# A hybrid attention block: which PSUM pool holds the weighted sums of the cross attention, and where Silu's table is loaded

## The chip, the cores and the metric

The kernel runs on one core of a Trainium2 chip. The metric is the device time of one launch in microseconds (us). The core has five engines with instruction queues of their own, each of which works strictly in order: TensorE (PE in the profile, with its weight loads as PEld), VectorE (DVE), ScalarE (ACT), GpSimdE (POOL) and SyncE (SP), which here issues the transfers.

## What is computed

One layer of an encoder on 1024 tokens of width 1024: a mixer (windowed attention and a gated delta rule), a cross attention of 4 heads into 256 memory tokens, and a SwiGLU feed-forward part. The change touches the cross attention alone:

```python
def _memory_cross_attention(h, mem_n, w_q, w_kv, w_o):
    q = (h @ w_q).reshape(b, s, CROSS_HEADS, CROSS_HEAD_DIM)
    kv = mem_n @ w_kv                       # k, v: 256 memory tokens, 4 heads of 256
    p = jax.nn.softmax(jnp.einsum('bqhd,bkhd->bhqk', q, k) * (CROSS_HEAD_DIM ** -0.5), axis=-1)
    o = jnp.einsum('bhqk,bkhd->bqhd', p, v).reshape(b, s, D_MODEL)
    return o @ w_o
```

All matrix products are made to almost float32 accuracy from float32r parts: an operand is split into a high part (a rounding cast, on ACT) and a low part (the source less the high part, on DVE or POOL), and a product is three matmuls, high x high, high x low and low x high.

## The kernel before

The sequence is worked in two halves of 512 tokens, `hf` 0 and 1; with 4 heads that makes 8 rounds (half, head), called heads 0 to 7 below. The helper `split` (L102 the high part, L103 the low part) and `load_w` (L127 the load into `wraw`, then the split into `whi` and `wlo`) serve everywhere.

For each round the loop calls `cross_q`, which makes q for one head (tile `pcq`, two column tiles of 24 matmuls 128x512, the dense product, L263), and then `cross_attention` for the round before. That has these steps on the way: scores into `pcs` (L1110, 24 matmuls 128x256, two tiles of 12 for two pairs of token tiles), row maxima (`cmx`, L1112 and L1113, DVE), exponentials (`cpr`, L1117, ACT), sums inverted and multiplied in (L1119, L1120, DVE), 8 transposes on PE into two tiles `pct` (L1126), their split into `cph` and `cpl`, the weighted sums `pco` (L1136, two tiles of 6 matmuls) and their split, which overwrites q. After the last round a Silu over a tile of 4 columns (L1151) makes ACT load the table of Silu, which the feed-forward part needs first at L1233. What follows is the output product `mid_gemm` with `w_co`, first for half 0 and then for half 1 (tile `pmg`, L1021, 192 matmuls each); its first lines load the gain `gpost` (L995) and multiply it by 32 on ACT (L996).

PSUM has eight banks, in three pools at this stage: `pg3`, tag `pg`, 4 banks, which `pcq` and `pmg` take in turn; `pn3`, tag `pn`, 2 banks, for the transposes `ptn` and `pct`; `px3`, tag `px`, 2 banks, for `pcs` and `pco`. A tile takes over a bank when the last reader of the tile before it is done.

The order of the work on each engine isn't written out: the framework's scheduler takes the instructions by priority (that is, by their place in the program, with loads of weights ahead) as soon as its model of time finds inputs, an engine and a buffer free, and fixes one order per engine when the kernel is built. Within a pool's tag, banks are given in the order of the requests. An edit of one line can therefore move instructions on every engine.

Of the kernel before, what the change touches and what calls it, by code (L numbers as in the profile page):

```python
# [10 lines left out]
F32 = mybir.dt.float32  # L11
F32R = mybir.dt.float32r
I32 = mybir.dt.int32
AF = mybir.ActivationFunctionType
# [5 lines left out]
P = 128  # L20
S = 1024
D = 1024
KT = D // P
# [52 lines left out]
def tile_hybrid_block(  # L76
# [6 lines left out]
    nc = tc.nc  # L83
# [9 lines left out]
    def f32(ap):  # L93
        return ap.bitcast(F32)

    def bc(ap, axis, shape):
        return ap.unsqueeze(axis).to_broadcast(list(shape))

    def split(hi, lo, src, scale=None, eng=None):

        if scale is None:
            nc.scalar.copy(hi, src)  # L102
            (eng or nc.vector).tensor_tensor(lo, src, f32(hi), ALU.subtract)  # L103
        else:
            nc.scalar.activation(hi, src, AF.Identity, scale=scale)
            nc.vector.scalar_tensor_tensor(lo, src, scale, f32(hi), ALU.mult, ALU.subtract)

    def pool(name, bufs, **kw):
        return tc.tile_pool(name=name, bufs=bufs, reuse_waits="tile", **kw)
# [84 lines left out]
    pg = pgs.enter_context(pool("pg", 3, space=PSUM))  # L194
# [769 lines left out]
    pg = p3.enter_context(pool("pg3", 4, space=PSUM))  # L964
    pn = p3.enter_context(pool("pn3", 2, space=PSUM, side="right"))
    px = p3.enter_context(pool("px3", 2, space=PSUM, side="right"))
# [132 lines left out]
    def cross_attention(q, h):  # L1099
        prs = []  # L1100
        mxs = tx.tile([P, 4], F32, tag="cmx", name="cmx")
        sums = tx.tile([P, 4], F32, tag="csum", name="csum")
        for tp in range(2):
            pp = px.tile([P, 2, ML], F32, tag="px", name="pcs")
            for t2_ in range(2):
                tt = slice((2 * tp + t2_) * P, (2 * tp + t2_ + 1) * P)
                for j in range(2):
                    ct = 2 * h + j
                    for i, (a, b_) in enumerate(((0, 0), (1, 0), (0, 1))):
                        nc.tensor.matmul(pp[:, t2_, :], q[a][:, ct, tt], kr_[b_][:, ct, :],  # L1110
                                         start=(j == 0 and i == 0), stop=(j == 1 and i == 2))
            nc.vector.tensor_reduce(mxs[:, 2 * tp:2 * tp + 2], pp, axis=AX.X, op=ALU.max)  # L1112
            nc.vector.tensor_scalar(mxs[:, 2 * tp:2 * tp + 2], mxs[:, 2 * tp:2 * tp + 2], -1.0 / 16.0, None, ALU.mult)  # L1113
            pr = tx.tile([P, 2, ML], F32, tag="cpr", name="cpr", bufs=4)
            for t2_ in range(2):
                n = 2 * tp + t2_
                nc.scalar.activation(pr[:, t2_, :], pp[:, t2_, :], AF.Exp, bias=mxs[:, n:n + 1], scale=1.0 / 16.0,  # L1117
                                     accum_out=sums[:, n:n + 1])
            nc.vector.reciprocal(sums[:, 2 * tp:2 * tp + 2], sums[:, 2 * tp:2 * tp + 2])  # L1119
            nc.vector.tensor_tensor(pr, pr, bc(sums[:, 2 * tp:2 * tp + 2], 2, (P, 2, ML)), ALU.mult)  # L1120
            prs.append(pr)
        pts = []
        for kt in range(2):
            pt = pn.tile([P, 512], F32, tag="pn", name="pct")
            for t in range(4):
                nc.tensor.transpose(pt[:, t * P:(t + 1) * P], prs[t // 2][:, t % 2, kt * P:(kt + 1) * P], ident)  # L1126
            ph = tx.tile([P, 512], F32R, tag="cph", name="cph", bufs=2)
            pl = tx.tile([P, 512], F32R, tag="cpl", name="cpl", bufs=2)
            split(ph, pl, pt)
            pts.append((ph, pl))  # L1130
        for j in range(2):
            po = px.tile([P, 512], F32, tag="px", name="pco")
            cs = slice((2 * h + j) * P, (2 * h + j + 1) * P)
            for kt in range(2):
                for i, (a, b_) in enumerate(((0, 0), (0, 1), (1, 0))):
                    nc.tensor.matmul(po, vr_[a][:, kt, cs], pts[kt][b_], start=(kt == 0 and i == 0),  # L1136
                                     stop=(kt == 1 and i == 2))
            split(q[0][:, 2 * h + j, :], q[1][:, 2 * h + j, :], po)
        return sums

    q0, behind = operand(opB, "s1"), None
    for hf in range(2):
        q = operand(opB, "s2") if hf else q0
        for h in range(4):
            cross_q(hf, q, h)
            if behind:
                cross_attention(*behind)
            behind = q, h
    q1 = q
    last = cross_attention(*behind)  # L1150
    nc.scalar.activation(last, last, AF.Silu)  # L1151
    L2.close()
    Lk.close()

# [87 lines left out]
    pg = L0.enter_context(pool("pg4", 8, space=PSUM))  # L1242
# [298 lines left out]
```

## Time and profile before

| what | value |
|---|---|
| median of 3 runs | 1548.82 us (1545.64 to 1549.28) |
| profiled execution | 1551.7 us, of which the profile's span is 1549.9 us |
| PE busy | 1494.9 us (96% of the span) |
| DVE / ACT / POOL busy | 1060.1 / 713.3 / 302.6 us |
| mean granted TensorE clock | 0.986 |
| scores `pcs` of the cross attention | from 671.7 to 859.5 us |
| weighted sums `pco` | from 713.9 to 869.5 us |
| Silu's table load | 1283 ns, at 863.1 us |

Times in the profile are counted from the start of the span. A row of the timeline gives the start, the length, the engine, the line, the operation with its output and inputs, the count of merged instructions, and in brackets the idle time before it with what ended it. A row of a table by stage gives for a stretch its length, then for each engine busy time and count, then the granted clock of TensorE, the share of the transfer engines and GB/s. A matmul's length overlaps with the next one's: dense matmuls 128x512 follow each other every 0.23 us, though each is listed with 0.39 us.

### The profile page before, as it was taken

How to read it: one execution, taken by the hardware profiler on the slowest of the kernel's cores; microseconds unless marked ns; L12 is line 12 of the kernel's file. 1: busy time of each engine (PE TensorE's matmuls, PEld its weight loads, DVE VectorE, ACT ScalarE, POOL GpSimd, SP SyncE). 2: the span in 40 equal slices, each digit the busy share in tenths (PEclk: the TensorE clock that was granted, in tenths of full speed). 3: DMA queues.
4: the chain of work that ended last, by engine and by line, in shares of the span. 5: the costliest groups of instructions: out<-in, count | busy, mean ns of one | idle time of the engine just before them, and what ended most of it. 6: DMA issues, size and time to landing. Idle time of an engine off the chain costs nothing.

```text
span 1549.9 us, 20928 instructions
## 1 busy us (share of the span) xinstructions
PE 1494.9 (96%) x7451; PEld 1257.4 (81%) x7451; DVE 1060.1 (68%) x1762; ACT 713.3 (46%) x1377; POOL 302.6 (20%) x297
## 2 busy tenths in 40 slices
PE   6999999988999999999999999999999999999998
PEld 5888887877899878888888777888888888888786
DVE  6877898756898766443346377786868554696676
ACT  5665552236556765454334554322323332454532
POOL 2000110000003202253202231443433433000010
PEclk9999999999999999999999999999999999999999
DMA  6244456767997585354223264344433334853355
GB/s 206 74 131 124 133 150 164 209 169 246 317 305 244 161 294 173 117 181 149 69 69 130 72 205 142 112 136 129 148 119 121 102 102 147 289 189 102 109 175 165
DMA packets 267366, 247.16 MB, mean 159 GB/s; under 512 B 39016, under 2 KB 204797, under 8 KB 267261
## 3 DMA queue, kind: packets, MB, share of 16 engines
q1 hardware_dynamic: 267261, 245.82, 50.8%
q8 instruction: 59, 0.97, 0.3%
q14 instruction: 46, 0.38, 0.1%
HBM read 173.65 MB, written 69.50 MB: 157 GB/s over the span
## 4 chain that ended last, share of the span: by engine, by line
PE 80%; DMA 7%; DVE 6%; ACT 3%; SPq 2%; issue 2%; POOL 1%; DVEq 0%; ACTq 0%; POOLq 0%
PE pg L263 13%; PE pmg L1021 9%; PE pD L1212 8%; PE pE L1212 8%; PE pA L1212 7%; PE pcq L263 6%; PE pdX L1402 6%; PE pdA L1402 4%; PE pB L1212 4%; PE psc L787 2%; PE pdD L1402 2%; PE pco L1136 1%; PE pcs L1110 1%; PE pdX L1495 1%; DVE wlo L103 1%
## 5 line engine op out<-in xcount | busy, mean ns | idle before, releaser
L102 ACT CAST whi<-wraw 128x1024 fp32r<-128x1024 f32 x108 | 113.4, 1050 | 149.7 <-PE pg L263 36.0
L263 PE MATMUL pg<-hhi,whi 128*128 128x512 f32 x352 | 142.1, 405 | 2.8 <-DVE rop L732 2.8
L263 PE MATMUL pg<-hlo,whi 128*128 128x512 f32 x352 | 141.0, 401 | 0.0
L263 PE MATMUL pg<-hhi,wlo 128*128 128x512 f32 x352 | 140.7, 400 | 0.0
L103 DVE TENSOR_TENSOR wlo<-wraw,whi 128x1024 fp32r<-128x1024 f32 x78 | 95.4, 1224 | 63.4 <-ACT whi L102 62.3
L1021 PE MATMUL pmg<-whi,b 128*128 128x512 f32 x384 | 118.6, 393 | 0.2 <-ACT b L102 0.2
L1212 PE MATMUL pA<-s,whi 128*128 128x512 f32 x352 | 109.5, 392 | 1.2 <-ACT m L1229 1.0
L103 POOL TENSOR_TENSOR wlo<-wraw,whi 128x1024 fp32r<-128x1024 f32 x30 | 72.3, 2411 | 146.6 <-ACT whi L102 146.4
L1021 PEld LDWEIGHTS pmg<-whi,b 128*128 128x128 f32 x384 | 71.5, 188 | 14.7 <-ACT b L102 0.6
L263 PEld LDWEIGHTS pg<-hhi,whi 128*128 128x128 f32 x352 | 67.8, 193 | 16.9 <-DVE rop L732 3.3
L263 PEld LDWEIGHTS pg<-hhi,wlo 128*128 128x128 f32 x352 | 68.0, 193 | 13.5
L263 PEld LDWEIGHTS pg<-hlo,whi 128*128 128x128 f32 x352 | 67.9, 193 | 13.4
L1212 PEld LDWEIGHTS pA<-s,whi 128*128 128x128 f32 x352 | 65.4, 188 | 15.2 <-ACT m L1229 1.5
L1402 PE MATMUL pdX<-dhl,whi 128*128 128x512 f32 x264 | 76.1, 390 | 1.5 <-DVE zv L1457 0.8
L1021 PE MATMUL pmg<-wlo,b 128*128 128x512 f32 x192 | 72.2, 391 | 0.0
L1212 PE MATMUL pA<-s,wlo 128*128 128x512 f32 x176 | 68.6, 391 | 1.8 <-DVE wlo L103 1.8
L102 ACT CAST whi<-araw 128x1024 fp32r<-128x1024 f32 (+1 forms) x36 | 35.3, 982 | 70.8 <-PE pdX L1402 27.6
L1289 POOL TENSOR_TENSOR act<-act,up 128x512 f32<-128x512 f32 x33 | 50.1, 1519 | 88.5 <-DVE up L1288 53.2
L103 DVE TENSOR_TENSOR wlo<-araw,whi 128x1024 fp32r<-128x1024 f32 (+1 forms) x36 | 40.8, 1133 | 38.7 <-ACT whi L102 36.2
L288 DVE SCALAR_TENSOR_TENSOR acc<-cp,cols,acc 128x1024 f32<-128x1024 f32 x48 | 61.4, 1281 | 1.5 <-ACT acc L286 0.8
L1402 PEld LDWEIGHTS pdX<-dhl,whi 128*128 128x128 f32 x264 | 49.3, 188 | 12.8 <-issue 1.1
L1262 DVE TENSOR_TENSOR sr<-sr,wraw 128x512 f32<-128x512 f32 x22 | 36.6, 1662 | 28.6 <-POOL sr L1261 28.6
(410 smaller groups left out, 3963.9 us busy)
## 6 DMA issues: line engine op xcount, KB each, us to landing
wraw<-in_w_gate_up_dram SPq DMA_DIRECT2D x52, 512.0 KB, 3.9
kv<-d_kv SPq DMA_DIRECT2D x32, 512.0 KB, 6.9
wraw<-in_w_in_dram SPq DMA_DIRECT2D x22, 512.0 KB, 4.9
b<-in_w_down_dram SPq DMA_DIRECT2D x20, 512.0 KB, 7.4
araw<-d_as SPq DMA_DIRECT2D x20, 512.0 KB, 3.9
pz<-d_pz SPq DMA_DIRECT2D x32, 256.0 KB, 7.1
wraw<-in_w_ckv_dram SPq DMA_DIRECT2D x16, 512.0 KB, 7.0
wraw<-in_w_out_dram SPq DMA_DIRECT2D x16, 512.0 KB, 3.9
```

The costliest lines, as they stand in the source:

```text
L102: nc.scalar.copy(hi, src)
L103: (eng or nc.vector).tensor_tensor(lo, src, f32(hi), ALU.subtract)
L263: nc.tensor.matmul(p_, w[:, k, :], ah[a][:, k, :], start=(k == 0 and i == 0), stop=(k == nk - 1 and i == 2))
L288: nc.vector.scalar_tensor_tensor(acc, cp[:, t:t + S], taps[t], acc, ALU.mult, ALU.add)
L787: nc.tensor.matmul(out[:, d, h, :], lt[:, d, h, :], rt[:, d, h, :], start=True, stop=True)
L1021: nc.tensor.matmul(pp[t], act[a][:, k, tt], w_[:, kk, :], start=(k == 0 and i == 0), stop=(k == KT - 1 and i == 2))
L1110: nc.tensor.matmul(pp[:, t2_, :], q[a][:, ct, tt], kr_[b_][:, ct, :], start=(j == 0 and i == 0), stop=(j == 1 and i == 2))
L1136: nc.tensor.matmul(po, vr_[a][:, kt, cs], pts[kt][b_], start=(kt == 0 and i == 0), stop=(kt == 1 and i == 2))
L1212: nc.tensor.matmul(out_, w[a][:, k, :], xx[b_][:, k, :], start=(start and k == 0 and i == 0), stop=(k == HK - 1 and i == 2), skip_group_ch ...
L1262: nc.vector.tensor_tensor(s[1], s[0], a_[:, 0:HK], ALU.subtract)
L1289: nc.gpsimd.tensor_tensor(o_, o_, up, ALU.mult)
L1402: nc.tensor.matmul(banks[t], a[:, k - k0, tt], w, start=(first and k == 0 and i == 0), stop=(k == NB - 1 and i == 2), skip_group_check=not ...
```

## The change

Two lines differ. The weighted sums take their bank from the pool `pg3`, the one of the dense products, where they took it from `px3`. And the small Silu reads the high part of the last column tile of q for half 1, which the last split of the last round writes; before, it read and wrote the sums of the softmax.

```diff
         for j in range(2):
-            po = px.tile([P, 512], F32, tag="px", name="pco")
+            po = pg.tile([P, 512], F32, tag="pg", name="pco")
             cs = slice((2 * h + j) * P, (2 * h + j + 1) * P)
...
     last = cross_attention(*behind)
-    nc.scalar.activation(last, last, AF.Silu)
+    nc.scalar.activation(last, f32(q1[0][:, KT - 1, 0:4]), AF.Silu)
```

PE executes the same matmuls and transposes in both. The first 3106 in the built programs stand in the same order, up to the scores of head 0 (685.6 us in the trace of before); then the orders differ up to the 4095th, in the middle of the second output product; from there on they are the same again. What the built programs show at three places follows. Numbers at the end of a tile's name tell tiles of one name apart; `x2` is a row that stands twice.

**ACT, the first round of the cross attention.** `ptn` are the transposes of half 1's normalized input and `s00` its high part; `cpr_6981` and `cpr_7001` are the exponentials of head 0, `cpr_7125` and `cpr_7145` those of head 1, `pcq_7048` and `pcq_7081` the dense product of head 2. Before:

```order
L105 ACTIVATE s00_6754<-ptn_6791,cols_73 128x512
L102 CAST whi_7188<-wraw_7186 128x1024
L102 CAST b0_6830<-pcq_7048 128x512
L105 ACTIVATE s00_6754<-ptn_6798,cols_73 128x512
L105 ACTIVATE s00_6754<-ptn_6805,cols_73 128x512
L102 CAST whi_7221<-wraw_7219 128x1024
L102 CAST b0_6830<-pcq_7081 128x512
L1117 ACTIVATE cpr_6981,csum_6965<-pcs_6966,cmx_6964 128x256 x2
L996 ACTIVATE gpost_8001<-gpost_8001 128x1024
L1117 ACTIVATE cpr_7001,csum_6965<-pcs_6986,cmx_6964 128x256 x2
```

With the change:

```order
L105 ACTIVATE s00_6754<-ptn_6791,cols_73 128x512
L105 ACTIVATE s00_6754<-ptn_6798,cols_73 128x512
L105 ACTIVATE s00_6754<-ptn_6805,cols_73 128x512
L996 ACTIVATE gpost_8001<-gpost_8001 128x1024
L1117 ACTIVATE cpr_6981,csum_6965<-pcs_6966,cmx_6964 128x256 x2
L1117 ACTIVATE cpr_7001,csum_6965<-pcs_6986,cmx_6964 128x256 x2
L1117 ACTIVATE cpr_7125,csum_7109<-pcs_7110,cmx_7108 128x256 x2
L102 CAST cph_7011<-pct_7006 128x512
L102 CAST cph_7020<-pct_7015 128x512
L1117 ACTIVATE cpr_7145,csum_7109<-pcs_7130,cmx_7108 128x256 x2
```

The casts of head 2's product are gone from between, and the scaling of `gpost` stands ahead of all exponentials of head 0. On PE the transposes `ptn_6784` to `ptn_6805` stand directly behind the scores of head 0, and behind them the scores of head 1 (`pcs_7110`, then `pcs_7130`), the transposes `pct` of head 0 and its first `pco`; the dense product of head 2 comes after these. On SP the load of `gpost` and four loads of `xr` stand ahead of the load of `wraw_7332`, which they followed before.

**PE, a round in the middle.** `pct_7294` and `pct_7303` are the transposes of head 2, `pcq_7659` belongs to head 6, `pcq_7338` to head 4. Before:

```order
L263 MATMUL pcq_7659<-s01_6755,whi_7655 128x512
L263 MATMUL pcq_7659<-s00_6754,wlo_7656 128x512
L1126 MATMUL pct_7294<-ident_68,cpr_7269 128x128 x2
L1126 MATMUL pct_7303<-ident_68,cpr_7269 128x128 x2
L263 MATMUL pcq_7659<-s00_6754,whi_7655 128x512
L263 MATMUL pcq_7659<-s01_6755,whi_7655 128x512
L1126 MATMUL pct_7294<-ident_68,cpr_7289 128x128 x2
L1126 MATMUL pct_7303<-ident_68,cpr_7289 128x128 x2
L263 MATMUL pcq_7659<-s00_6754,wlo_7656 128x512
```

With the change:

```order
L1110 MATMUL pcs_7420<-kr0_6007,b0_6830 128x256
L1110 MATMUL pcs_7420<-kr0_6007,b3_6831 128x256
L1110 MATMUL pcs_7420<-kr1_6008,b0_6830 128x256
L1126 MATMUL pct_7294<-ident_68,cpr_7269 128x128 x2
L1126 MATMUL pct_7303<-ident_68,cpr_7269 128x128 x2
L1126 MATMUL pct_7294<-ident_68,cpr_7289 128x128 x2
L1126 MATMUL pct_7303<-ident_68,cpr_7289 128x128 x2
L1136 MATMUL pco_7312<-cph_7299,vr0_6009 128x512
L1136 MATMUL pco_7321<-cph_7299,vr0_6009 128x512
L263 MATMUL pcq_7338<-s00_6754,whi_7334 128x512
```

Before, the dense products run some four heads ahead and stand between all steps of a head, and in half 1 the output product of half 0 takes that place. With the change the 16 scores that are left of head 2 and all 24 of head 3 stand in a row of 40, the transposes of head 2 and two of its weighted sums follow at once, and the dense product is at most two heads ahead. This pattern comes for heads 2 and 3, 4 and 5, and 6 and 7. No matmul of the output product stands among the scores any more; its first 21 come just before the last ten `pco` of head 7.

**DVE and ACT, the last rounds.** `pcs_7832` and `pcs_7852` are the scores of head 6, `pcs_7910` and `pcs_7930` those of head 7, `pcq_7803` the last dense product, `wlo_8049` a weight of the output product. DVE with the change:

```order
L1112 TENSOR_REDUCE cmx_7830<-pcs_7832 128x2
L103 TENSOR_TENSOR wlo_8049<-wraw_8046,whi_8048 128x1024
L103 TENSOR_TENSOR b2_7331<-pcq_7803,b1_7330 128x512
L1113 TENSOR_SCALAR cmx_7830<-cmx_7830 128x2
L1112 TENSOR_REDUCE cmx_7830<-pcs_7852 128x2
```

ACT before:

```order
L102 CAST whi_8540<-wraw_8538 128x1024
L1151 ACT_TABLE_LOAD
L1151 ACTIVATE csum_7909<-csum_7909 128x4
L102 CAST cph_7955<-pct_7950 128x512
L102 CAST cph_7964<-pct_7959 128x512
L102 CAST b1_7330<-pco_7968 128x512
L102 CAST b1_7330<-pco_7977 128x512
```

ACT with the change:

```order
L102 CAST cph_7955<-pct_7950 128x512
L102 CAST cph_7964<-pct_7959 128x512
L102 CAST b1_7330<-pco_7968 128x512
L102 CAST b1_7330<-pco_7977 128x512
L1151 ACT_TABLE_LOAD
L1151 ACTIVATE csum_7909<-b1_7330 128x4
L102 CAST whi_8078<-wraw_8076 128x1024
```

The table load moved from ahead of the casts of head 7's transposes to behind the last cast of its weighted sums. On DVE the low part of a weight stands between the first maximum of head 6 and the step that scales it.

## The prediction

> **What bounds the kernel now.** I read the busy times first, then the chain of work that ended last.
>
> ```profile
> PE 1494.9 (96%) x7451; PEld 1257.4 (81%) x7451; DVE 1060.1 (68%) x1762; ACT 713.3 (46%) x1377; POOL 302.6 (20%) x297
> PE 80%; DMA 7%; DVE 6%; ACT 3%; SPq 2%; issue 2%; POOL 1%; DVEq 0%; ACTq 0%; POOLq 0%
> ```
>
> TensorE is the bound, so the change counts by the idle time it gives PE or takes from it; the matmuls are the same. Next the table by stage, over the stretch in which the orders differ:
>
> ```profile
> 686.81:838.10 151.29, 151.29 (x757) 127.83 (x756) 68.98 (x112) 63.55 (x131) 32.98 (x24) 1.00 0.30 98
> 848.20:853.60 5.40, 3.97 (x19) 2.53 (x17) 2.47 (x4) 2.31 (x5) 0.00 (x0) 1.00 0.51 184
> 853.60:862.70 9.10, 9.06 (x52) 7.76 (x52) 4.49 (x10) 3.08 (x10) 0.00 (x0) 1.00 0.00 0
> 862.70:865.10 2.40, 0.63 (x4) 0.42 (x4) 1.42 (x2) 2.37 (x5) 0.00 (x0) 1.00 0.00 0
> 865.10:868.50 3.40, 3.34 (x8) 2.62 (x9) 1.29 (x2) 0.50 (x2) 0.00 (x0) 0.50 0.54 159
> 868.50:890.00 21.50, 21.50 (x112) 17.86 (x111) 6.57 (x8) 15.00 (x29) 10.19 (x8) 1.00 0.23 75
> ```
>
> For 151 us, nearly the whole cross attention, PE has no gap: the dense products cover every step of the softmax. Any new wait there is paid in full, and nothing is to be won. What can be won lies in the last rounds: 1.4 us idle in the second row, 1.8 in the fourth, 0.1 in the others, and 3.4 us at half clock, which cost 1.7. Together 5.0 us. The timeline tells why:
>
> ```profile
> 847.81 1.03 PE L1126 MATMUL pct<-ident,cpr 128*128 128x128 f32 x8
> 849.41 0.73 PE L1136 MATMUL pco<-cph,vr 128*128 128x512 f32 x2 [0.56 <-ACT cph L102]
> 850.78 0.50 PE L1136 MATMUL pco<-cpl,vr 128*128 128x512 f32 x1 [0.64 <-DVE cpl L103]
> 863.04 0.63 PE L1126 MATMUL pct<-ident,cpr 128*128 128x128 f32 x4 [0.39 <-DVE cpr L1120]
> 865.16 1.22 PE L1136 MATMUL pco<-cph,vr 128*128 128x512 f32 x2 [1.49 <-ACT cph L102]
> 862.07 1.05 ACT L102 CAST whi<-wraw 128x1024 fp32r<-128x1024 f32 x1
> 863.14 1.28 ACT L1151 ACT_TABLE_LOAD   x1
> 864.43 0.20 ACT L1151 ACTIVATE csum<-csum 128x4 f32<-128x4 f32 x1
> 864.54 1.05 ACT L102 CAST cph<-pct 128x512 fp32r<-128x512 f32 x2
> ```
>
> The table load keeps ACT from the last `cph`, and PE waits 1.49 us. These rows also show what `pco` costs where no dense work stands between transposes and sums: about 0.6 us from the start of `cph` to `pco` (864.54 to 865.16).
>
> **The change, part by part.**
>
> The table load now stands behind the last cast. There it delays the casts of the next weights by 1.5 us; PE has 27 dense matmuls before it needs them, 6.2 us at 0.23 each (eight in 1.98 us, the row below), so it costs nothing; without that cover it would cost its 1.5 us. The 1.49 us wait and probably its half clock go.
>
> ```profile
> 889.60 1.98 PE L1021 MATMUL pmg<-whi,b 128*128 128x512 f32 x8
> ```
>
> The pool is the larger part. A `pco` tile now stands in the queue for the four banks of the dense product, which can no longer run ahead, and the new order puts PE's scores and transposes next to each other. What such a neighbourhood costs is the time of the softmax chain, which the trace shows for a covered head:
>
> ```profile
> 722.09 3.04 PE L1110 MATMUL pcs<-kr,b 128*128 128x256 f32 x24
> 723.72 0.69 DVE L1112 TENSOR_REDUCE cmx<-pcs 128x2 f32<-128x512 f32 x1 [1.85 <-PE pcs L1110]
> 724.45 0.17 DVE L1113 TENSOR_SCALAR cmx<-cmx 128x2 f32<-128x2 f32 x1
> 724.71 0.47 ACT L1117 ACTIVATE cpr<-pcs,cmx 128x256 f32<-128x256 f32 x1 [3.57 <-DVE cmx L1113]
> 725.53 0.20 ACT L1117 ACTIVATION_READ_ACCUMULATOR cpr<-pcs,cmx 128x1 f32 x1
> 725.97 0.69 DVE L1120 TENSOR_TENSOR cpr<-cpr,csum 128x512 f32<-128x512 f32 x1
> ```
>
> A score takes 0.12 us (24 in 2.9). The first tile of 12 is issued at 723.5 and its exponentials end at 725.73: a score bank is held 2.2 us beyond its last score. Two banks serve the scores.
>
> *The first round.* The rows of before:
>
> ```profile
> 685.62 1.44 PE L1110 MATMUL pcs<-kr,b 128*128 128x256 f32 x10
> 686.19 1.41 DVE L106 SCALAR_TENSOR_TENSOR s<-ptn,cols,s 128x512 fp32r<-128x512 f32 x2
> 697.80 1.03 PE L987 MATMUL ptn<-ident,xr 128*128 128x128 f32 x8
> 698.44 1.27 ACT L105 ACTIVATE s<-ptn,cols 128x512 fp32r<-128x512 f32 x2 [3.62 <-PE ptn L987]
> 698.54 0.34 SPq L995 DMA_DIRECT2D gpost<-in_g_cross_post_dram  x1
> 703.95 1.06 ACT L996 ACTIVATE gpost<-gpost 128x1024 f32<-128x1024 f32 x1 [1.88 <-DMA gpost<-in_g_cross_post_dram]
> 704.91 0.45 ACT L1117 ACTIVATE cpr<-pcs,cmx 128x256 f32<-128x256 f32 x1
> ```
>
> Up to 686.8 nothing differs. Then 16 transposes follow in a row on two banks; ACT (0.6 each) and DVE (0.7) free a bank at about 687.0, 687.6, 689.1 and 689.7, so PE ends at 690.2 where the work is 1.9 us: 1.5 lost. Head 1's scores need head 0's bank, and head 0's exponentials now stand on ACT behind the scaling of `gpost`. Its load is issued when the last transposes have read `xr`, as in before (698.54, while the last eight run): about 690.0. It lands 5.4 us later (698.54 to 703.95), so the scaling starts at 695.4, the exponentials at 696.4 (0.96 on, as 703.95 to 704.91) and end at 697.4; PE waits from 690.2 to 697.5, 7.3 us. Without the load DVE's chain (four more L106, two maxima, to 692.5) would let the exponentials end at 693.5. Then 22 scores and 8 transposes run with little wait, and `pco` waits 0.65 for `cph`, which stands behind head 1's exponentials. Sum 9.4. After 7 us idle I count one stretch of half clock, of which 1.5 us fall on work: 10.9. Bounds for the load: the quickest landing of a load of this size near it is 3.5 us, the slowest 7.5 (below), so 1.9 less to 2.1 more; I take the same transfer's 5.4.
>
> *The middle.* These rows give the neighbours in the queues:
>
> ```profile
> L103 DVE TENSOR_TENSOR b<-pcq,b 128x512 fp32r<-128x512 f32 x13 | 9.0, 690 | 17.2 <-ACT b L102 17.2
> L102 ACT CAST whi<-wraw 128x1024 fp32r<-128x1024 f32 x20 | 21.0, 1051 | 11.5 <-PE pcq L263 4.9 <-issue 4.8 <-PE pmg L1021 1.8
> L103 DVE TENSOR_TENSOR wlo<-wraw,whi 128x1024 fp32r<-128x1024 f32 x10 | 12.2, 1224 | 7.0 <-ACT whi L102 6.6
> L102 ACT CAST cph<-pct 128x512 fp32r<-128x512 f32 x12 | 6.4, 590 | 15.8 <-PE pct L1126 15.8
> DMA to landing us min/median/max: 3.5/3.5/7.5
> ```
>
> In a row of 40 scores the first tile of the even head is done after 8 (1.0 us), the second after 16 (1.9). The odd head needs the first bank at 1.9; it is free 2.2 us after 0.95, so at 3.15, and later by 0.6 because DVE has the split of `pcq` between the maximum and its scaling: PE waits 1.2 to 1.85 us, and I take 1.85, since the order shows the split there. The 24 scores then last longer than the chain of the even head, the transposes don't wait, and `cph` comes 0.56 us late behind the odd head's exponentials. That makes 2.4 us, for heads 2/3 and 4/5: 4.8. In odd heads (1, 3, 5) the transposes have dense work ahead of them; `whi` and the cast of `pcq` precede `cph` on ACT, some 0.4 each: 1.2. Sum 6.0.
>
> *The last rounds.* Heads 6/7 have the same row of scores, but on DVE also a `wlo` of 1.2 us ahead of the scaling: 3.05. No dense product is left to put between: `cph` 0.5, `cpl` behind two maxima and a multiplication 1.3, the second `cph` behind two casts of `pco` 1.0. Sum 5.8; one stretch of half clock, 1.7: 7.5.
>
> Behind that I add nothing. Half 0's output product is now normalized while PE works on half 1's, which before had the softmax of half 1 for cover:
>
> ```profile
> 838.24 0.68 DVE L1025 TENSOR_TENSOR z<-pmg,gpost 128x512 f32<-128x512 f32 x1
> 839.70 1.28 DVE L1035 SCALAR_TENSOR_TENSOR z<-z,prs,xr 128x1024 f32<-128x1024 f32 x1
> 843.11 0.75 DVE L1044 TENSOR_SCALAR xr<-z,pr 128x1024 f32<-128x1024 f32 x1 [0.73 <-POOL pr L164]
> ```
>
> From the last L1025 to the last L1044 it takes 5.6 us there. The new order has two L1035 and three L1044 in that place, 6 to 7 us, and PE has 45 matmuls (10.3 us) and 7 transposes before the last piece; without enough cover it would be some 1 us.
>
> The half clock rests on the row 865.10 above: after waits of 0.39 and 1.49 within 2.4 us the granted clock is 0.50 for 3.4 us. [...]
>
> **Sum**: 10.9 + 6.0 + 7.5 - 5.0 = 19.4 us slower. The profiled execution took 1551.7 us (span 1549.9) and would take 1571.1; it lies 2.9 above the median, so the median goes from 1548.8 to 1568.
>
> **The rivals.**
>
> *Early landing, full clock* (slower by 11 to 13). The `gpost` load lands soon enough for DVE to set the end (3.9 less) and no half clock follows (3.2 less): 19.4 - 7.1 = 12.3, or 1561; with the 1.2 of the middle, 1560. For it: a clock window may lie so that a wait of 1.85 falls in two. Against it: the measured 5.4, and 7.3 us idle.
>
> *Full clock in middle and tail.* A mechanism in which only a gap as long as the first one halves the clock: 1.7 less, 1566. Against it stands the row 865.10. [...]
>
> *Half clock after every wait* (slower by 24 to 29). Each of the two rows of 40 scores, and the tail twice, brings a stretch: 3 x 1.7 more, 19.4 + 5.1 = 24.5, or 1573; with a landing at 7.5 us, 1575, and with a further stretch at an odd head 1577. For it: transposes and waits alternate as they did at 862. Against it: 848.20 to 853.60 has 1.4 us idle and the full clock behind it.
>
> *The tail decides* (faster). The score banks, freed of `pco`, come back before PE asks, and the dense products still cover the softmax; then only the tail's 5.0 us go: 1543.8. This decides if a bank is held no longer than PE takes for the other bank's scores, 1.0 us in the middle; the chain of 2.2 us speaks against it, as does the order, with no dense matmul among the 40.
>
> *No change to be seen*: new waits of about 5 us in all, so that they pay for the tail. It needs the first round to cost under 3, against the 5.5 that it costs even with the load landed early.
>
> **Chances.** The sum as it stands 0.57, full clock in middle and tail 0.10, early landing 0.12, half clock after every wait 0.11, no change 0.06, faster 0.04. A measurement can tell about 0.3% (4.6 us) from no change: faster 0.04, same 0.06, slower 0.90. The likeliest one's own range is 1562 to 1573; with most of the neighbouring cases, 1558 to 1577.
>
> **What would show it.** In the profile after: PE idle some 7 us before `pcs`, released by ACT `cpr` L1117, around 690 to 698, and ACT waiting for the transfer of `gpost` before it; two waits near 1.9 us and one near 3 before `pcs`, same releaser; short waits of `pco` for `cph`; granted clock below 1.00 behind the first and the last; the table load behind the last cast with no wait of PE on it. The forecast is wrong if PE runs without gaps from 690 to 840, or if `gpost` lands before 692.

## The result, and the profile after

The changed kernel takes 1568.59 us (median of 4, 1568.09 to 1569.51); the kernel before, run beside it, 1547.23 us (1544.33 to 1549.28). The ratio is 1.0139 with a 95% interval of 1.0122 to 1.0155: slower, by 21 us between the medians. The profiled execution took 1568.1 us with a span of 1566.4, so it lies 0.5 us below the median, where that of the kernel before lay 2.9 above the median given with it. The spans differ by 16.5 us.

First the busy times and the chain of work that ended last, by engine, of the changed kernel:

```profile
PE 1496.1 (96%) x7451; PEld 1259.7 (80%) x7451; DVE 1060.2 (68%) x1762; ACT 713.8 (46%) x1377; POOL 304.4 (19%) x297
PE 82%; DVE 6%; DMA 6%; ACT 2%; issue 2%; SPq 2%; POOL 1%; DVEq 0%; ACTq 0%; POOLq 0%
```

At this distance nothing is to be seen: the shares hardly moved, and PE is the bound as before. The cross attention has to be looked at by itself. Its start and end are two rows of PE's timeline, the ten scores of head 0 and the first product of the feed-forward part. The first two rows are of the changed kernel:

```profile
684.49 1.44 PE L1110 MATMUL pcs<-kr,b 128*128 128x256 f32 x10
...
919.47 0.62 PE L1212 MATMUL pA<-s,whi 128*128 128x512 f32 x2
```

The second of them in the kernel before (its first row, at 685.62, is shown in the prediction):

```profile
900.80 0.74 PE L1212 MATMUL pA<-s,whi 128*128 128x512 f32 x2 [0.16 <-DVE z L1025]
```

The stage went from 215.2 to 235.0 us: 19.8 longer, where the sum said 19.4. The spans differ by less because the profiled execution was 1.1 us ahead when the stage began, and because the rest behind it ran 2.2 us shorter (of that, 1.8 is one wait of a `pA` product for `wlo` that the kernel before had at 904.3).

The waits of PE in the stage, added up by what released them (us in all, how often, the longest), changed kernel:

```profile
PE pcs L1110 <- ACT cpr L1117: 13.9, 4, 5.9
PE pco L1136 <- ACT cph L102: 2.1, 5, 0.5
PE ptn L987 <- DVE s L106: 0.9, 1, 0.9
PE pco L1136 <- DVE cpl L103: 0.4, 1, 0.4
```

The stage of the kernel before had no wait of scores for exponentials at all. The table by stretch shows where they lie (columns as in the prediction: length, then busy time and count of PE, weight loads, DVE, ACT, POOL, then the granted clock):

```profile
685.40:702.00 16.60, 9.52 (x55) 8.19 (x54) 9.24 (x20) 7.87 (x20) 1.00 (x1) 0.79 0.54 191
702.00:732.00 30.00, 30.00 (x144) 25.03 (x143) 8.19 (x15) 9.77 (x17) 7.17 (x3) 1.00 0.18 53
732.00:743.00 11.00, 7.86 (x47) 7.25 (x46) 8.48 (x17) 5.38 (x20) 2.37 (x1) 0.84 0.16 49
743.00:772.00 29.00, 29.00 (x139) 24.15 (x138) 6.99 (x12) 8.61 (x15) 7.17 (x3) 1.00 0.16 47
772.00:784.00 12.00, 8.87 (x60) 7.85 (x59) 9.24 (x19) 5.88 (x20) 2.37 (x1) 1.00 0.21 64
784.00:813.00 29.00, 28.22 (x139) 23.58 (x137) 8.87 (x12) 9.37 (x14) 4.80 (x2) 1.00 0.19 55
813.00:836.00 23.00, 19.85 (x97) 16.70 (x98) 11.69 (x25) 9.76 (x26) 0.00 (x0) 0.93 0.07 24
836.00:880.00 44.00, 44.00 (x196) 36.46 (x195) 20.52 (x21) 17.23 (x31) 9.35 (x12) 1.00 0.37 130
```

Four places are idle, and nothing between them: the first round, heads 2/3 (732 to 743), heads 4/5 (772 to 784), and the end with heads 6/7. The old tail's idle time is gone (836 to 880 is full). PE's waits are 17.3 us where the same stage had 3.5 before, so 13.8 of the 19.8. A second part is the clock. It was at 0.50 here:

```profile
693.00:699.80 6.80, 4.46 (x21) 4.46 (x22) 2.58 (x6) 3.38 (x12) 0.00 (x0) 0.50 0.67 269
737.30:740.70 3.40, 3.40 (x19) 3.40 (x18) 1.70 (x4) 1.02 (x4) 0.00 (x0) 0.50 0.07 21
815.80:819.20 3.40, 3.40 (x19) 3.40 (x18) 1.76 (x5) 0.97 (x5) 0.00 (x0) 0.51 0.09 33
```

PE worked for 11.26 us in these stretches and would have needed half: 5.6 us, against 1.7 before, 3.9 more. Waits and clock make 17.7 of the 19.8; about 2 us of PE's own time in the stage are left over, and where they lie stays open.

### The profile page after: what moved, and what is told of

Read it like the earlier page. It is cut to its first block, busy times and chain, and to the rows that moved or that the text cites. A ratio compares the mean times of both kernels' runs of the same rounds, so it can differ in the third digit from the quotient of the medians.

```text
span 1566.4 us, 20940 instructions
## 1 busy us (share of the span) xinstructions
PE 1496.1 (96%) x7451; PEld 1259.7 (80%) x7451; DVE 1060.2 (68%) x1762; ACT 713.8 (46%) x1377; POOL 304.4 (19%) x297
## 4 chain that ended last, share of the span: by engine, by line
PE 82%; DVE 6%; DMA 6%; ACT 2%; issue 2%; SPq 2%; POOL 1%; DVEq 0%; ACTq 0%; POOLq 0%
PE pg L263 12%; PE pmg L1021 10%; PE pD L1212 8%; PE pE L1212 8%; PE pA L1212 7%; PE pcq L263 6%; PE pdX L1402 6%; PE pdA L1402 4%; PE pB L1212 4%; PE psc L787 3%; PE pdD L1402 2%; PE pcs L1110 2%; PE pco L1136 1%; PE pdX L1495 1%; PE pck L918 1%
## 5 line engine op out<-in xcount | busy, mean ns | idle before, releaser
L103 DVE TENSOR_TENSOR wlo<-wraw,whi 128x1024 fp32r<-128x1024 f32 x78 | 95.2, 1221 | 82.3 <-ACT whi L102 81.4
L1021 PE MATMUL pmg<-whi,b 128*128 128x512 f32 x384 | 115.0, 391 | 0.0
L103 POOL TENSOR_TENSOR wlo<-wraw,whi 128x1024 fp32r<-128x1024 f32 x30 | 72.4, 2412 | 184.4 <-ACT whi L102 184.4
L103 DVE TENSOR_TENSOR wlo<-araw,whi 128x1024 fp32r<-128x1024 f32 (+1 forms) x36 | 40.8, 1134 | 39.5 <-ACT whi L102 39.5
```

The costliest lines, as they stand in the source:

```text
L1021: nc.tensor.matmul(pp[t], act[a][:, k, tt], w_[:, kk, :], start=(k == 0 and i == 0), stop=(k == KT - 1 and i == 2))
```

## The experiments

The first theory is the prediction's: the change of pool costs, because `pco` stands in the queue of the dense product's banks, and then scores, transposes and sums stand next to each other and the softmax chain lies bare; Silu's line gains a little. Its main rival is that something in the new order costs by itself (the load of `gpost`, DVE's queue) and the pool is only the occasion. All times are medians beside runs of the kernel before on the same chip; that kernel's median was 1547.23 beside the change, 1549.47 beside the maxima with a PSUM operand, 1548.89 beside Silu's line, the pool, `gpost` loaded late and the tensor operation, and 1549.55 beside the other four. The length of the stage is measured between the same two rows in each trace:

| kernel | time, us | ratio to before (95%) | stage, us |
|---|---|---|---|
| before | 1547.23 to 1549.55 | 1 | 215.2 |
| the change | 1568.59 | 1.0139 (1.0122 to 1.0155) | 235.0 |
| Silu's line alone | 1546.10 | 0.9984 (0.9969 to 0.9998) | 212.8 |
| the pool alone | 1570.88 | 1.0150 (1.0134 to 1.0167) | 236.4 |
| the change, `gpost` loaded late | 1565.15 | 1.0114 (1.0098 to 1.0131) | 231.7 |
| the change, maxima scaled by a tensor operation | 1568.35 | 1.0135 (1.0120 to 1.0149) | 234.8 |
| the change, maxima scaled with a PSUM operand | 1566.00 | 1.0109 (1.0090 to 1.0129) | 231.4 |
| the change, maxima scaled on ACT | 1558.70 | 1.0061 (1.0046 to 1.0077) | 224.0 |
| Silu's line, sums in the transposes' banks | 1541.84 | 0.9959 (0.9943 to 0.9975) | 208.6 |
| the same, `gpost` loaded late | 1542.57 | 0.9958 (0.9941 to 0.9974) | 208.6 |
| Silu's line, maxima scaled on ACT | 1547.63 | 0.9987 (0.9976 to 0.9999) | 214.4 |

**Silu's line alone.**

```
 before, with
-    nc.scalar.activation(last, last, AF.Silu)
+    nc.scalar.activation(last, f32(q1[0][:, KT - 1, 0:4]), AF.Silu)
```

> The kernel before with the second line of the change alone: Silu reads the last column tile of q, so its table is loaded behind the last cast. Theory (the load only held ACT ahead of the last cph): the wait of 1.49 us of pco for cph at 865 falls to about 0.65, and the half clock behind it goes, so 0.9 to 2.6 us faster than before; the rest of the order stays. Rival (the load was hidden, the tail is set by the chain of the last head): no difference, below 0.5 us.

Measured: 2.8 us faster by the medians, 2.4 us by the stage. The timeline of its tail:

```profile
862.73 0.73 PE L1136 MATMUL pco<-cph,vr 128*128 128x512 f32 x2 [0.46 <-ACT cph L102]
867.31 1.28 ACT L1151 ACT_TABLE_LOAD   x1
```

The wait of 1.49 us is 0.46, and no stretch of the stage has a granted clock below 1.00 any more. The wait that went (1.0) and the half clock (1.7) make 2.7, close to what was measured.

**The pool alone.**

```
 before, with
-            po = px.tile([P, 512], F32, tag="px", name="pco")
+            po = pg.tile([P, 512], F32, tag="pg", name="pco")
```

> The kernel before with the first line of the change alone: the weighted sums take banks of the dense products. Theory (the banks carry the whole loss): 20 to 24 us slower than before, that is the whole change's 21 plus 1 to 1.5 for the table load, which in this order stands between two casts of head 6's sums with nothing to cover it; waits of PE for the exponentials of 6, 2.6, 2.6 and 2.7 us as in the changed kernel. Rival (the place of the table load takes part in the new order of PE): clearly less than 15 us slower.

Measured: 22.0 us slower by the medians, 21.2 by the stage. The two parts nearly add up: by the stage 21.2 less 2.4 is 18.8, and the whole change cost 19.8 there. Its waits in the stage, and the place of the table load, which still stands ahead of the casts of head 7:

```profile
PE pcs L1110 <- ACT cpr L1117: 14.0, 4, 6.0
PE pco L1136 <- ACT cph L102: 3.5, 5, 2.0
```

```profile
820.34 1.28 ACT L1151 ACT_TABLE_LOAD   x1
...
822.86 0.73 PE L1136 MATMUL pco<-cph,vr 128*128 128x512 f32 x2 [2.03 <-ACT cph L102]
```

The four waits of the scores are those of the whole change, to 0.1 us. So they belong to the pool.

**The gain loaded late.** The load of `gpost` and its scaling are issued behind the last weight load of the stage; the order of the matmuls stays but for two scores of head 7.

```
 the change, with
-    gp = gpost_tile(tz, g_cross_post)
+    with tc.issue_after(wloads[-1].ins):
+        gp = gpost_tile(tz, g_cross_post)
```

> The changed kernel, with the load of gpost for the cross attention put behind the last load of weights of the dense product on SP, so that ACT no longer waits for it ahead of head 0's exponentials; PE's order is the same but for two scores of head 7. Theory (the load sets the end of the first wait): the first wait of pcs for the exponentials falls from 5.9 to about 3.0 us, the end that DVE's chain allows, and the half clock behind it gets shorter, so 3 to 5 us less than the changed kernel, 16.5 to 18.5 slower than before. Rival (the exponentials wait for their maxima anyway): no difference from the changed kernel.

Measured: 3.3 us less in the stage than with the whole change, 1565.15 us, which is 16.3 slower than before. The start of head 0's exponentials and the first round's wait, from its timeline:

```profile
689.58 0.47 ACT L1117 ACTIVATE cpr<-pcs,cmx 128x256 f32<-128x256 f32 x1 [1.23 <-DVE cmx L1113]
690.65 4.39 PE L1110 MATMUL pcs<-kr,b 128*128 128x256 f32 x22 [3.03 <-ACT cpr L1117]
```

5.94 became 3.03. So half of the first wait was the load on ACT, and the other half is DVE's chain behind the transposes: the exponentials now start when the scaled maxima (`cmx`) are there. The main rival had a part of the time, but only where PE already waited for head 0's exponentials.

**The maxima scaled in another form.** In the middle the changed kernel had something that no row of before had led me to expect. Timeline of heads 2/3, changed kernel:

```profile
732.21 2.37 POOL L103 TENSOR_TENSOR wlo<-wraw,whi 128x1024 fp32r<-128x1024 f32 x1 [3.05 <-ACT whi L102]
732.83 0.68 DVE L103 TENSOR_TENSOR b<-pcq,b 128x512 fp32r<-128x512 f32 x1
733.42 1.17 DVE L1113 TENSOR_SCALAR cmx<-cmx 128x2 f32<-128x2 f32 x1
735.22 0.17 DVE L1113 TENSOR_SCALAR cmx<-cmx 128x2 f32<-128x2 f32 x1
735.76 4.26 PE L1110 MATMUL pcs<-kr,b 128*128 128x256 f32 x24 [2.63 <-ACT cpr L1117]
```

The scaling of two columns took 1.17 us, not 0.17, and it ends at 734.59, 0.01 us after POOL's split of a weight (732.21 + 2.37 = 734.58). The split of `pcq`, which ran on DVE in between, took its usual 0.68. The first idea was that the form of the operation (a scalar operation in place) makes DVE yield to POOL; a multiplication of two tensors would not.

```
 the change, with (scale16 a constant tile, sc16 in the profile)
-  nc.vector.tensor_scalar(mxs[...], mxs[...], -1.0 / 16.0, None, ALU.mult)
+  nc.vector.tensor_tensor(mxs[...], mxs[...], scale16, ALU.mult)
```

> The changed kernel, with the scaling of the maxima (L1113) as a product of two tensors where it was a product with a constant; same size, same place in every order. In the changed kernel two of the sixteen scalings take 1.17 us where the others take 0.17, both while POOL splits a weight, and both end with POOL's instruction. Theory (this form of instruction is held while POOL works, the form with two tensors is not): all sixteen take 0.2 us, the two waits of 2.6 us fall to 1.6, and the kernel takes 2 to 3.7 us less than the changed one. Rival (whatever DVE does there is held): the two stay at 1.2 us and the time stays the same.

Measured: no difference, 1568.35 us, and the row is the same:

```profile
732.11 2.36 POOL L103 TENSOR_TENSOR wlo<-wraw,whi 128x1024 fp32r<-128x1024 f32 x1 [3.04 <-ACT whi L102]
733.33 1.16 DVE L1113 TENSOR_TENSOR cmx<-cmx,sc 128x2 f32<-128x2 f32 x1
```

That theory fell: both forms are held. What the held operations have in common is that all their operands lie in SBUF, while the split of `pcq` reads PSUM. That is the next theory.

**The maxima scaled with a PSUM operand.**

```
 the change, with
-  nc.vector.tensor_scalar(mxs[...], mxs[...], -1.0 / 16.0, None, ALU.mult)
+  nc.vector.scalar_tensor_tensor(mxs[...], pp[:, :, 0], 0.0, mxs[...], ALU.mult, ALU.subtract)
 (the 1/16 goes into the split of the keys, one operation ahead of the stage, and the exponential's scale is 1)
```

> Kernel: the changed kernel in the same order on every engine, but the scaling of the maxima (L1113) has a column of the scores' PSUM tile among its operands: it computes 0 * score - maximum, and the 1/16 is put into the split of the keys instead, one operation of the stage before. Theory (DVE is held by POOL's 2.4 us split only where all operands of its operation lie in SBUF): L1113 takes at most 0.3 us, not 1.17, and the two waits in the rows of 40 scores fall from 2.6 to about 1.6 us; with no half clock behind them the gain is up to 3.5. So 1 to 4 us less than the changed kernel: 16 to 19 us slower than before. Rival (any small operation of DVE is held, wherever its operands lie): L1113 takes 1.17 us at the two places still, waits of 2.6 us, 19 to 21 us slower than before.

Measured: the stage is 3.6 us shorter than with the change; 1566.00 us, 16.5 slower than before. All 16 scalings in one row (shortest, median, longest in ns), then heads 2/3:

```profile
L1113 DVE SCALAR_TENSOR_TENSOR cmx<-pcs,cmx x16: 148/158/160, 692.9 to 820.4; 128x2 f32<-128x2 f32 x16
```

```profile
733.83 2.37 POOL L103 TENSOR_TENSOR wlo<-wraw,whi 128x1024 fp32r<-128x1024 f32 x1 [3.04 <-ACT whi L102]
735.05 0.15 DVE L1113 SCALAR_TENSOR_TENSOR cmx<-pcs,cmx 128x2 f32<-128x2 f32 x1
736.37 3.14 PE L1110 MATMUL pcs<-kr,b 128*128 128x256 f32 x24 [1.60 <-ACT cpr L1117]
```

In the same place, beside the same operation of POOL, with the same order on every engine, it took 0.15 us, and PE's wait went from 2.63 to 1.60. The wait of heads 4/5 went by as much (the four waits add up to 12.1, not 13.9), and the stretch of half clock at 737 is gone. 2 x 1.0 + 1.7 = 3.7, as measured. The theory holds. Its operation has a third form, which could be the reason in place of the operand; against that stands L1035, of the same form with its operands in SBUF: in the trace of the changed kernel it took 2.82 us at 661.18, beside POOL's split, and 1.28 elsewhere. By the times alone the kernel's interval still touches that of the change; it is the trace that decides here.

**The maxima scaled on ACT.**

```
 the change, with
-  nc.vector.tensor_scalar(mxs[...], mxs[...], -1.0 / 16.0, None, ALU.mult)
+  nc.scalar.mul(mxs[...], mxs[...], -1.0 / 16.0)
```

> Kernel: the changed kernel with the scaling of the maxima (L1113) on ACT and not on DVE. Theory (an operation of DVE with all its operands in SBUF is held while POOL works on a split of 2.4 us): ACT scales in some 0.2 us, so in the two rows of 40 scores the wait of PE falls from 2.6 to about 1.6 us each; in the last row DVE's split of a weight no longer stands ahead of the scaling, 2.75 to about 1.5. The order also puts the scaling of gpost behind head 0's first exponentials, so that one score bank comes free without it: 5.9 to about 4. Together 4 to 6 less than the changed kernel: 13 to 16 us slower than before. Rival (the scaling of 1.17 us only stands beside POOL's split by chance, and the bank's release is set elsewhere): the waits in the middle stay at 2.6 us and only the first round gains, 17 to 19 us slower than before.

Measured: 9.2 us slower than before, where the theory said 13 to 16 and the rival 17 to 19: on the theory's side, but outside its range too. Two of its waits of scores, and the list of the stage:

```profile
688.99 4.42 PE L1110 MATMUL pcs<-kr,b 128*128 128x256 f32 x24 [1.92 <-ACT cpr L1117]
...
728.09 1.71 PE L1110 MATMUL pcs<-kr,b 128*128 128x256 f32 x12 [1.11 <-ACT cpr L1117]
```

```profile
PE pcs L1110 <- ACT cpr L1117: 5.3, 4, 1.9
PE pco L1136 <- ACT cph L102: 3.0, 5, 1.1
```

The first wait is 1.92 (4 expected), since a score bank comes free ahead of `gpost`; the other three are 1.1 each (1.5 to 1.6 expected), as the scaling also stands no more behind DVE's split of `pcq` or of a weight. Three of the four 3.4 us stretches of half clock went with them, which I had not counted. Since the order differs a little too, this run shows how much the chain is worth, not the hold alone; for that there is the run with the PSUM operand.

**Sums in the transposes' banks.** Is it any second user of a pair of banks that costs, or the queue of the dense product?

```
 before, with Silu's new line and
-            po = px.tile([P, 512], F32, tag="px", name="pco")
+            po = pn.tile([P, 512], F32, tag="pn", name="pco")
```

> Kernel: before, with Silu's new line and the tiles of the weighted sums in the two banks of the transposes and not in those of the scores or the dense products. Theory (what costs is the queue of the dense products' banks, which the changed kernel gives to the sums): the dense products run ahead again, every row of scores has dense matmuls beside it, no wait of PE for cpr over 1 us, and the tail has dense matmuls between its sums: the 5.0 us of the old tail go, 3 to 5 us faster than before, 1544 to 1546. Rival (any second user of a pair of banks costs as much): the transposes wait for the split of the sums, 0.5 to 1 us at each of eight heads, 0 to 4 us slower than before.

Measured: 1541.84 us, 7.7 us faster than before, beyond the 3 to 5 expected. Its order keeps dense products between the steps (in the traces the longest row of PE instructions without one is 36 here, 28 in the kernel before and 70 with the change), and the trace has no wait of PE in the stage:

```profile
683.13:836.00 152.87, 152.87 (x800) 130.84 (x799) 73.50 (x127) 66.19 (x143) 25.90 (x11) 1.00 0.25 78
836.00:880.00 44.00, 44.00 (x211) 36.54 (x210) 21.36 (x23) 25.80 (x47) 22.71 (x24) 1.00 0.50 176
880.00:891.72 11.72, 11.72 (x54) 9.69 (x52) 4.72 (x5) 4.20 (x9) 2.09 (x5) 1.00 0.54 165
```

PE is full for 208.59 us from the first row of the stage to the last, at full clock. The sums left the scores' banks here as they did in the change; only the queue in which they stand now is another one. So the cost of the change comes with the dense product's banks and the order that is built for them; no run has that order with other banks, so these two are not told apart. This kernel beats both others. The stage is 6.6 us shorter: 5.2 of that are the waits (3.5) and the half clock (1.7) of the kernel before, and where the other 1.4 come from stays open.

**The same with the gain loaded late.**

```
 the kernel above, with
-    gp = gpost_tile(tz, g_cross_post)
+    with tc.issue_after(wloads[-1].ins):
+        gp = gpost_tile(tz, g_cross_post)
```

> Kernel: the one before in this list (sums in the transposes' banks, Silu's new line), with the load of gpost issued behind the last of the weight loads. Theory (the load costs only where no dense product covers head 0's exponentials): no difference to the same kernel without it, within 2 us, since 19 dense matmuls stand ahead of the sums there. Rival (the scaling of gpost holds ACT in any order): 2 to 4 us faster than the kernel with the early load.

Measured: 1542.57 us, and a stage of the same 208.6 us. The scaling of `gpost` stands ahead of head 0's second pair of exponentials in the kernel with the early load:

```profile
701.04 1.06 ACT L996 ACTIVATE gpost<-gpost 128x1024 f32<-128x1024 f32 x1 [1.47 <-DMA gpost<-in_g_cross_post_dram]
702.01 0.45 ACT L1117 ACTIVATE cpr<-pcs,cmx 128x256 f32<-128x256 f32 x1
```

It costs nothing there, because dense products cover the exponentials. The same load cost 2.9 us of wait in the changed kernel: the price is the missing cover, not the load.

**The maxima on ACT, with cover.** Silu's new line and the scaling on ACT, everything else as before.

> Kernel: before with Silu's new line and the scaling of the maxima on ACT. Theory (the hold of DVE by POOL costs only where PE waits for the chain of the softmax): the dense products cover that chain here, so no difference to the kernel with Silu's line alone beyond what the slightly other order of the tail brings: 1 to 5 us faster than before. Rival (ACT, now with 16 more operations ahead of its casts, is late for the transposes): 1 to 4 us slower than before.

Measured: 1547.63 us, against 1546.10 with Silu's line alone, each beside its own runs of before: ratios of 0.9987 and 0.9984, no difference to be seen. The profiled stage is 1.6 us longer than with Silu's line alone, and its tail has a stretch of half clock (850.39 to 853.80, which cost 1.7) that the other has not. Where the chain is covered, no gain from scaling the maxima on ACT can be seen.

## Why the prediction was right, and which terms were off

The predicted 1568 us and the sign came out, and by the mechanism that was given; but several terms were off by 1 to 2 us in both directions and cancelled, so that the total came this close is luck. For the predicted 19.4 us the medians show 21.4, the spans 16.5 and the stage 19.8.

*The first round*: 10.9 predicted, 9.3 measured. The row of 16 transposes cost 0.90 (1.5 predicted), the scores waited 5.94 (7.3), `pco` 0.22 (0.65), half clock 2.2 (1.5). The rows on the load:

```profile
689.10 0.34 SPq L995 DMA_DIRECT2D gpost<-in_g_cross_post_dram  x1
693.32 1.06 ACT L996 ACTIVATE gpost<-gpost 128x1024 f32<-128x1024 f32 x1 [3.20 <-DMA gpost<-in_g_cross_post_dram]
695.34 4.84 PE L1110 MATMUL pcs<-kr,b 128*128 128x256 f32 x22 [5.94 <-ACT cpr L1117]
```

Most of what was mis-sized in the wait is the landing: 4.2 us, not the 5.4 of the same transfer in the kernel before, but inside the bounds of 3.5 to 7.5. That without the load PE would wait for DVE's chain alone was put at 3.3 us (690.2 to 693.5), and the run with the late load measured 3.03. The rival of an early landing named the right direction but asked for a landing soon enough for DVE to decide, and full clock; neither came.

*The middle*: 6.0 predicted, 8.0 measured. Each row of 40 scores was given 1.85 for the bank and 0.56 for `cph`; measured were 2.63 and 0.51, then 2.62 and 0.51. The chain itself was right, rather too long: with a PSUM operand the wait is 1.60, inside the bounds of 1.2 to 1.85. What failed is that the duration of L1113 was taken from a place where POOL was idle (0.17 us). The odd heads were to wait 0.4 each, 1.2 in all, and waited for nothing (702 to 732 and 743 to 772 are full). And one stretch of half clock came, 1.7, where none was counted.

*The last rounds*: 7.5 predicted, 5.6 measured: 2.75 for 3.05, and 1.2 for the three waits of `pco` that were put at 2.8 (0.28, 0.37 and 0.53). Each had been made to wait for all that stands ahead of it in its queue; how much of that was done by then was not tested by itself. The half clock came as counted.

Together that is 9.3 + 8.0 + 5.6 - 5.0 = 17.9 for the predicted 19.4; the 2 us of PE's own time that were left over above make up the 19.8.

*The table load and what follows*: right. It stands at 834.28, no wait of PE follows it, and the 44 us behind the last weighted sum are full; the old tail's 5.0 us went. Silu's line alone showed 2.4 to 2.8 us of them.

*The clock*: 0.50 three times where the forecast had it twice, 5.6 us in all for its 3.2. Between the two rivals on it, neither held: the first gap and the tail were followed by half clock, one of two equal gaps in the middle was, the other not. A gap of 2.63 us was enough here, ahead of the scores at 735.76.

## What to carry to other kernels

A change of a tile's pool can change the order in which the scheduler lets work run ahead: before a short-lived tile is put beside the tiles of the covering work, look at the built order for places where the covering work disappears from between dependent steps, and price these with the chain of a covered step. If a second user has to go somewhere, try the banks of a step that stands in the same chain; here that was worth 26 us of the stage against the banks of the dense product. A duration may be carried from one place of a trace to another only with a look at what POOL does beside it: here L1113 took 0.17 us beside an idle POOL and 1.17 beside its split.

## What the runs showed of the hardware that was not expected

**DVE was held by POOL's split of a weight.** The scaling by a constant and the operations on two tensors, with operands in SBUF alone, were held when they started well before that split ended, whatever their size (128x2 to 128x1024): 1.17 us for two columns in place of 0.17, to the end of POOL's operation. The kernel before had one such row that I had passed over, on a larger operation (0.69 us elsewhere), and beside it one that was not held:

```profile
700.74 2.39 POOL L103 TENSOR_TENSOR wlo<-wraw,whi 128x1024 fp32r<-128x1024 f32 x1 [3.95 <-ACT whi L102]
702.10 0.17 DVE L1119 RECIPROCAL csum<-csum 128x2 f32<-128x2 f32 x1 [0.23 <-ACT cpr L1117]
702.30 1.38 DVE L1120 TENSOR_TENSOR cpr<-cpr,csum 128x512 f32<-128x512 f32 x1
```

POOL ends at 703.13, and the multiplication then runs for 0.55 us more. Between 600 and 930 us of the eleven traces all 13 scalings in SBUF (L1113) that started beside such a split were held, and all 11 of the larger operations L1035; of 362 operations that read PSUM (L1112, L103 on `pcq`, L1113 with a PSUM operand and others) none was, and none of seven reciprocals. The forms with two tensors took 1.16 us (L1113 as a tensor operation) and 1.38 us (the multiplication above) where they were held. Why the scaling by a constant, with one tensor as input, was held and the reciprocal (0.17 us at 702.10), also with one and also in SBUF, was not, no run here shows.

**The granted clock went by more than the length of a gap.** Gaps of 2.63 and 2.62 us in the same execution, ahead of the same kind of row of scores, were followed by half clock and by none; with the late load it was the second that was. The 1.49 us gap in the old tail, with one of 0.39 ahead of it, was followed by it, gaps of 1.60 and 1.11 in the middle were not. Every half clock in this stage lasted 3.4 us or twice that. The places where it begins have the same step: in the trace of the changed kernel they are 692.96, 737.33 and 815.84, that is 44.37 and then 78.51 us apart, 13 and 23 times 3.413. Over the whole span of that trace half clock begins eleven times, first at 256.05 and last at 1563.35, which is 383 such steps, and the other nine stand on them to within 0.01 us; so do the nine of the kernel before (257.52 to 1544.35) among themselves. What fits, as a reading of these places, is a grid of fixed stretches of this length, in which a gap may fall whole or in two. On this grid the two equal gaps of the changed kernel fall differently:

```profile
733.91:737.33 3.42, 1.57 (x13) 1.57 (x14) 2.94 (x7) 1.93 (x8) 0.66 (x1) 1.00 0.45 135
771.46:774.87 3.41, 2.00 (x17) 1.79 (x15) 2.33 (x4) 1.47 (x2) 2.34 (x1) 1.00 0.40 121
774.87:778.28 3.41, 2.20 (x18) 2.20 (x19) 2.94 (x8) 1.93 (x8) 0.02 (x1) 1.00 0.53 159
```

PE was idle for 1.85 us of the first stretch, and half clock follows it; the second gap is cut in two, with 1.41 and 1.21 us idle, and none follows. Over this stage in the eleven traces, half clock followed all 20 grid stretches in which PE was idle for 1.81 us or more, and of the others (at most 1.78) only one, with 1.59 us, in the kernel with Silu's line and the maxima on ACT. So what counted here was, with that one exception, whether PE was idle for about half of a stretch; no run moved a gap on purpose.
